# A hybrid state-space and attention layer on one core: the second block's row work moved ahead, its accumulators paired in two banks

## The chip, the cores and the metric

The kernel runs on one core of one Trainium2 chip. The time is device microseconds of one execution. Before the change three runs gave 1505.21, 1506.19 and 1507.15 us, median 1506.19. One execution was also taken by the hardware profiler; the numbers of the trace come from that one.

## The reference

One layer over 2048 rows of width 1024. The part that the change touches is the first: the rows are normalised and multiplied by the input weights, and the first 512 output columns (u) feed a state-space branch.

```python
hn = rmsnorm(h, mix_norm_g[i])
proj = hn @ w_in[i]
u, g_ssm, q, k, v, g_attn = jnp.split(proj, SPLITS, axis=-1)
y_ssm = s5_branch(u, ...)                     # diagonal complex scan, GELU, GLU
y_ssm = y_ssm * jax.nn.silu(g_ssm)
y_att = stick_breaking_branch(q, k, v, q_norm_g[i], k_norm_g[i]) * jax.nn.silu(g_attn)
h = h + jnp.concatenate([y_ssm, y_att], axis=-1) @ w_out[i]
ple_gate = jax.nn.sigmoid(rmsnorm(h, ple_norm_g[i]) @ w_ple_gate[i])
h = h + ple_gate * (p[i] @ w_ple_proj[i])
```

`rmsnorm` divides each row by the root of its mean square. All matrix products of the first phase are done in float32 split into a high and a low part: high by high, high by low, low by high, three matmuls for one product.

## The kernel before

**Stages.** `phase_u` computes u for all rows. A middle stage follows, in which the state-space batches (`ssm_pack`, `ssm_batch`), the gates (`gate_unit`) and the first attention projections are interleaved. Then come attention over four pairs of heads, the gated linear unit, and the two output products.

**phase_u.** The 2048 rows are taken in eight blocks T of 256 rows, each in two halves (hf) of 128. For each block the rows are needed transposed and split (tile `xt`), four accumulators `ps[ct]` take 24 matmuls each (8 column chunks by three parts, L541 to L543), and each is copied into `uq`.

- Block 0 comes from an input that already lies transposed (`load_plain`). It is not normalised before the product. Instead `norms(i)`, once for each half, squares the rows (L575), adds them up on POOL (L577) and with a matmul by ones (L579), raises the mean to -1/2 on POOL (L581), and spreads the factor along a row with a diagonal matrix `dg` and a second matmul (L585), which is copied to `row` (L586). Block 0's accumulators are multiplied by `row` on DVE when they are copied out.
- Blocks 1 to 7 are read as rows by `load_x(T)`: DMA into a tile `x` (L593), squares with a sum on ACT into `jk` (L596), the power on POOL (L507), scaling by it on ACT (L598), 16 transposes of 64 rows on PE (L526) into the two banks `z0` and `z1` (`ps_x`), and the split on ACT (L513, high) and DVE (L65, low). Their accumulators are copied out by ACT alone (L635).
- Four `x` tiles exist (`XB` is 4). The plain tiles of block 0 take two of them, block 1 the other two. Block 2 gets block 0's two, once the L579 matmuls have read them.

**Banks.** The accumulators of T=0 and of all later blocks lie in the banks `w0`, `w1`, `o` and `acc`, one each, 256 of 512 columns used. The row-factor matmuls use `tr` and `ssm`.

**What sets the order.** The code is only recorded. `arrange` then runs a list scheduler (`plan`, `list_schedule`, `best_order`) with its own durations, several turns, and fixes the order of the rows on each engine. `e.first()` pulls the rows recorded in it to the front of the ranking; `e.later(k)` makes the DMAs in it wait in the ranking for the place `e.mark(k)`. At equal rank, the program's order counts. The DMAs stand in the queue of SP. DVE also carries a long chain of small preparation operations for the state-space tables (`cm`, `tabs`, `pr_...`), which the scheduler threads between the splits.

## Time and profile before

| | |
|---|---|
| median of three runs | 1506.19 us (1505.21 to 1507.15) |
| the profiled execution's own time | 1509.53 us |
| its span, first to last instruction | 1507.8 us |
| granted TensorE clock, mean | 0.991 |
| ACT busy in 40 to 50 us | 7.48 of 10 us |
| DMA share in 30 to 40 us | 0.92 (338 GB/s) |

A timeline row reads: start, duration, engine, line, operation, tile written <- tiles read, shape, count, and in brackets the idle time of that engine just before, with what ended it. Rows with a count are merged. Start times of neighbouring matmuls are closer than their durations, since matmuls overlap; the step from one start to the next is what one costs in a stream.

### The profile page before, as it was taken

What the parts mean: (1) busy time and instruction counts of PE and PEld (TensorE: products, weight loads), DVE (VectorE), ACT (ScalarE), POOL (GpSimd) and SP (SyncE); (2) the same over time, 40 slices, a digit from 0 to 9 for tenths busy, and PEclk for the clock granted to TensorE, in tenths of its full rate; (3) what the DMA queues carried; (4) which work ended last, traced back from release to release, by engine and by line L of the source; (5) the groups of instructions that cost most, each with busy time, mean ns of one, the idle gap of its engine ahead of it and who ended that gap; (6) DMA issues with size and microseconds to landing.
All of it is one profiled execution on the core that took longest, in us unless ns stands there. A gap on an engine that the chain in (4) does not pass through costs nothing.

```text
span 1507.8 us, 33560 instructions
## 1 busy us (share of the span) xinstructions
PE 1455.0 (96%) x13068; PEld 1219.8 (81%) x13068; DVE 1012.1 (67%) x1802; ACT 810.9 (54%) x1764; POOL 483.4 (32%) x524
## 2 busy tenths in 40 slices
PE   5999999999999999999999989999998999999998
PEld 5999989988888888887888777787776888777776
DVE  8944878967667876676767775546687557744544
ACT  5654545566556765565655555646554435533332
POOL 3121354422212112211111343531245554433433
PEclk9999999999999999999999999999999999999999
DMA  8876736645333433334333577743376546423221
GB/s 290 285 270 231 228 131 199 192 156 190 118 113 129 149 111 109 126 119 128 107 116 123 163 231 205 222 147 93 105 243 216 177 162 203 154 65 112 76 68 58
DMA packets 178909, 238.21 MB, mean 158 GB/s; under 512 B 65744, under 2 KB 121024, under 8 KB 167616
## 3 DMA queue, kind: packets, MB, share of 16 engines
q1 hardware_dynamic: 176368, 227.49, 46.9%
q0 software_dynamic: 2384, 8.59, 2.0%
q8 instruction: 103, 1.69, 0.4%
q14 instruction: 54, 0.44, 0.1%
HBM read 166.94 MB, written 64.90 MB: 154 GB/s over the span
## 4 chain that ended last, share of the span: by engine, by line
PE 75%; DVE 11%; issue 5%; DMA 4%; ACT 3%; POOL 1%; SPq 0%; POOLq 0%; DVEq 0%; ACTq 0%
PE ps_q L745 20%; PE ps_o L843 7%; PE ps_z L812 6%; PE ps_wt L526 4%; PE ps_g L707 3%; PE ps_g L709 3%; PE ps_g L708 3%; PE ps_h L709 3%; PE ps_h L707 3%; PE ps_h L708 3%; DMA wst<-in_ssm_w_glu_dram 2%; PE ps_u L541 1%; PE ps_u L543 1%; PE ps_u L542 1%; PE ps_sg L541 1%
## 5 line engine op out<-in xcount | busy, mean ns | idle before, releaser
L821 DVE TENSOR_TENSOR_SCAN px<-px,ps_z 128x512 f32<-128x512 f32 (+3 forms) x320 | 338.9, 1085 | 112.0 <-ACT px L816 59.4
L745 PE MATMUL ps_q<-w_w,xt 64*128 64x512 f32 x2784 | 378.3, 401 | 0.0
L745 PEld LDWEIGHTS ps_q<-w_w,xt 64*128 64x128 f32 x2784 | 265.6, 186 | 44.8 <-DVE qn L65 0.9
L835 ACT ACTIVATE ws<-ps_wt 128x512 f32<-128x512 f32 (+3 forms) x320 | 160.3, 538 | 81.2 <-PE ps_wt L526 80.8
L816 ACT ACTIVATE px<-ps_z 128x512 f32<-128x512 f32 (+3 forms) x320 | 159.8, 535 | 68.3 <-PE ps_z L812 66.7
L812 PE MATMUL ps_z<-k,q 64*128 64x512 f32 (+3 forms) x960 | 140.7, 382 | 6.1 <-DVE px L821 5.9
L843 PE MATMUL ps_o<-ws,v 128*64 128x128 f32 x2176 | 137.1, 278 | 0.7 <-ACT ws L835 0.7
L507 POOL TENSOR_TENSOR rs_qk<-rs_qk,mhalf 128x4 f32<-128x4 f32 x64 | 67.6, 1057 | 208.7 <-DVE rs_qk L72 192.9
L843 PEld LDWEIGHTS ps_o<-ws,v 128*64 128x64 f32 x2176 | 118.8, 138 | 19.1 <-issue 13.9
L526 PEld LDWEIGHTS ps_wt<-ident,px 64*128 64x128 f32 x2176 | 96.7, 139 | 30.4 <-ACT ws L835 8.3
L526 PE MATMUL ps_wt<-ident,px 64*128 64x64 f32 x2176 | 103.1, 225 | 6.3 <-ACT ws L835 4.3
L812 PEld LDWEIGHTS ps_z<-k,q 64*128 64x128 f32 x960 | 87.4, 187 | 25.0 <-DVE px L821 8.0
L819 POOL TENSOR_SCALAR_AFFINE_SELECT px<-px 128x128 f32<-128x128 f32 x128 | 38.7, 312 | 169.0 <-ACT px L816 145.6
L541 PE MATMUL ps_u<-xt,w_w 128*128 128x256 f32 x256 | 75.0, 295 | 8.4 <-ACT w_w L491 7.0
L1015 POOL TENSOR_TENSOR sg<-sg,h 128x512 f32<-128x512 f32 x32 | 44.9, 1413 | 114.7 <-DVE sg L65 114.7
L756 POOL TENSOR_TENSOR v<-qn,v 128x128 f32<-128x128 f32 x64 | 30.3, 473 | 154.1 <-DMA v<-qn 133.2
L543 PE MATMUL ps_u<-xt,w_w 128*128 128x256 f32 x256 | 73.8, 294 | 2.6 <-DVE w_w L76 2.6
L65 DVE TENSOR_TENSOR yr<-sx,yr 128x512 fp32r<-128x512 f32 x64 | 52.9, 847 | 34.3 <-ACT yr L513 33.5
L542 PE MATMUL ps_u<-xt,w_w 128*128 128x256 f32 x256 | 74.3, 291 | 0.5 <-DVE xt L65 0.5
L65 DVE TENSOR_TENSOR qn<-ps_q,part 128x512 f32<-128x512 f32 x54 | 36.9, 683 | 45.4 <-ACT part L751 41.4
L513 ACT ACTIVATE yr<-sx 128x512 fp32r<-128x512 f32 x64 | 39.2, 628 | 52.1 <-POOL sx L901 20.7
L541 PEld LDWEIGHTS ps_u<-xt,w_w 128*128 128x128 f32 x256 | 50.9, 199 | 9.5 <-ACT w_w L491 7.6
(418 smaller groups left out, 3470.2 us busy)
## 6 DMA issues: line engine op xcount, KB each, us to landing
xt<-hn SPq DMA_DIRECT2D x58, 1024.0 KB
hn<-xt SPq DMA_DIRECT2D x16, 1024.0 KB
h<-h SPq DMA_DIRECT2D x64, 256.0 KB
wst<-in_w_in_dram SPq DMA_DIRECT2D x48, 256.0 KB
xg<-hn SPq DMA_DIRECT2D x12, 1024.0 KB
out_dram<-sg SPq DMA_DIRECT2D x32, 256.0 KB
x<-in_x_dram SPq DMA_DIRECT2D x14, 512.0 KB
h<-in_x_dram SPq DMA_DIRECT2D x28, 256.0 KB
```

The lines of the kernel that those rows point to most:

```text
L65: nc.vector.tensor_tensor(out, a, b, op=op)
L526: e.nc.tensor.transpose(ps[h][:, 64 * k:64 * k + 64], v[r], e.ident[r, r])
L541: mm(out, wh, xh, start=first, stop=False)
L707: mm(out, xh, wh, start=first, stop=False, skip_group_check=more)
L708: mm(out, xh, wl, start=False, stop=False, skip_group_check=more)
L709: mm(out, xl, wh, start=False, stop=last, skip_group_check=more)
L745: nc.tensor.matmul(o, xt[r, a, c], A.w[c][r, b], start=c + s == 0, stop=c == NC8 - 1 and s == 2)
L812: nc.tensor.matmul(z[:, :n], q[half[h], a], A.k[ch][half[h], b, :n], start=s == 0, stop=s == 2)
L816: nc.scalar.activation(px[:, :n], z[:, :n], AF.Sigmoid, scale=-(HD ** -0.5))
L821: nc.vector.tensor_tensor_scan(rv, rv, z[:, :n][:, ::-1], initial=1.0 if carry[h] is None else carry[h], op0=ALU.mult, op1=ALU.bypass)
L835: nc.scalar.activation(dst, ps, AF.Copy, bias=1.0, scale=-1.0)
L843: nc.tensor.matmul(po[half[h], :P], A.v[sb][:, h], w[:, h, b], start=sb == i, stop=sb == 0)
```

## The change

`load_x(1)` is called ahead of `norms(0)` and `norms(1)`. The row-factor matmuls go to the banks `z0` and `z1`, which the transposes use too. Block 1's four accumulators lie two to a bank, columns 0 to 255 and 256 to 511, in `tr` and `ssm`; the other blocks keep their four banks. No operation is added or taken away.

```diff
-        ps = e.bank("ps_row", "tr", "ssm")
+        ps = e.bank("ps_row", "z0", "z1")
         nc.tensor.matmul(ps[:, :1], x[:, 0], ones[:, :1], start=True, stop=True)
...
-        ps = e.bank("ps_row", "tr", "ssm")
+        ps = e.bank("ps_row", "z0", "z1")
         nc.tensor.matmul(ps[:, :P], ones, d, start=True, stop=True)
...
         xts[0], w = load_plain(0)
+        with e.later(0):
+            xts[1] = load_x(1)
         norms(0)
         norms(1)
-        with e.later(0):
-            xts[1] = load_x(1)
...
-        ps = [e.bank("ps_u", "w0", "w1", "o", "acc", *(("z0", "z1") if T < 1 else ()))[:, :256] for _ in range(4)]
+        if T == 1:
+            ps = [b[:, h:h + 256] for b in [e.bank("ps_u1", "tr", "ssm") for _ in range(2)] for h in (0, 256)]
+        else:
+            ps = [e.bank("ps_u", "w0", "w1", "o", "acc")[:, :256] for _ in range(4)]
```

The scheduler then sets another order. In these rows the number behind a tile's name tells its copies apart. Block 1's rows are `x_284` and `x_316` before and `x_258` and `x_290` after; block 2's are `x_886` and `x_918` in both; block 3's are `x_1055` and `x_1087` before, `x_1053` and `x_1085` after. Lines from L620 on have moved by 3 in the changed file, so the copy L635 is L638 there.

**PE at the opening of block 1.** Before, where the last products of block 0 give way to block 1 (the dots stand for more transposes of the same tiles):

```order
L543 MATMUL ps_u_784<-xt_188,w_w_250 128x256
L585 MATMUL ps_row_267<-dg_265,ones_186 128x128
L579 MATMUL ps_row_274<-ones_186,x_190 128x1
...
L585 MATMUL ps_row_280<-dg_278,ones_186 128x128
...
L541 MATMUL ps_u_950<-xt_283,w_w_197 128x256
L542 MATMUL ps_u_950<-xt_283,w_w_197 128x256
```

After the change:

```order
L526 MATMUL ps_x0_299<-ident_141,x_290 128x64
L526 MATMUL ps_x1_300<-ident_141,x_290 128x64
L579 MATMUL ps_row_326<-ones_186,x_189 128x1
L541 MATMUL ps_u1_950<-xt_257,w_w_197 128x256
L579 MATMUL ps_row_339<-ones_186,x_190 128x1
L542 MATMUL ps_u1_950<-xt_257,w_w_197 128x256
...
L585 MATMUL ps_row_332<-dg_330,ones_186 128x128
L541 MATMUL ps_u1_950<-xt_257,w_w_218 128x256
```

All four row-factor matmuls stood ahead of block 1's products, one of them (for `x_189`) inside block 0. Now they stand behind both groups of block 1's transposes, and the second L579 and both L585 inside block 1's first accumulator.

**ACT from block 1 to block 2.** Before:

```order
L596 ACTIVATE jk_920,ss_921<-x_918 128x1024
L598 ACTIVATE x_886<-x_886,rs_x_891 128x1024
L596 ACTIVATE jk_1057,ss_1058<-x_1055 128x1024
L635 ACTIVATE uq_777<-ps_u_950 128x16x16
L598 ACTIVATE x_918<-x_918,rs_x_923 128x1024
L513 ACTIVATE xt_885<-ps_x0_895 128x8x64
L513 ACTIVATE xt_885<-ps_x1_896 128x8x64
L635 ACTIVATE uq_778<-ps_u_951 128x16x16
```

After the change, with the semaphores that a row waits for:

```order
L638 ACTIVATE uq_777<-ps_u1_950 128x16x16 [waits PE_49]
L638 ACTIVATE uq_778<-ps_u1_950 128x16x16
L598 ACTIVATE x_886<-x_886,rs_x_891 128x1024 [waits Activation_49,Pool_49]
...
L638 ACTIVATE uq_779<-ps_u1_951 128x16x16 [waits PE_49]
L638 ACTIVATE uq_780<-ps_u1_951 128x16x16
L596 ACTIVATE jk_1055,ss_1056<-x_1053 128x1024 [waits DMAHW1_49,DVE_49,Activation_49]
L598 ACTIVATE x_918<-x_918,rs_x_923 128x1024 [waits Pool_49]
L596 ACTIVATE jk_1087,ss_1088<-x_1085 128x1024 [waits DMAHW2_49,DVE_49,Activation_49]
L513 ACTIVATE xt_885<-ps_x0_927 128x8x64 [waits PE_49]
L513 ACTIVATE xt_885<-ps_x1_928 128x8x64 [waits PE_49]
L598 ACTIVATE x_1053<-x_1053,rs_x_1058 128x1024 [waits Pool_49]
```

The scaling of block 2's first half stood ahead of block 1's copies and that of its second half behind the first copy. Now the first stands behind two copies and the second behind all four.

**PE between block 1 and block 2.** Before, the last product of block 1 and the first of block 2 were neighbours:

```order
L542 MATMUL ps_u_953<-xt_283,w_w_250 128x256
L543 MATMUL ps_u_953<-xt_283,w_w_250 128x256
L541 MATMUL ps_u_1119<-xt_885,w_w_197 128x256
L542 MATMUL ps_u_1119<-xt_885,w_w_197 128x256
L543 MATMUL ps_u_1119<-xt_885,w_w_197 128x256
```

After the change (each group of transposes has 16 rows, of which the first is shown):

```order
L542 MATMUL ps_u1_951<-xt_257,w_w_250 128x256
L543 MATMUL ps_u1_951<-xt_257,w_w_250 128x256
L526 MATMUL ps_x0_927<-ident_141,x_918 128x64
...
L526 MATMUL ps_x0_1062<-ident_141,x_1053 128x64
...
L541 MATMUL ps_u_1117<-xt_885,w_w_197 128x256
L542 MATMUL ps_u_1117<-xt_885,w_w_197 128x256
```

The transposes of block 2's second half, and those of block 3's first half, now stand between the two. From the first product of block 3 the count of PE's rows is the same in both programs.

On SP the loads of block 2's rows stood right behind the two writes of block 0's rows (`hn0`, `hn1`); now each stands behind a write of block 1's rows (`hn2`, `hn3`). On POOL the power for block 1's first half stood third behind the long additions and now stands first, ahead of the rest of `norms(1)`. On DVE the second split of block 2 now stands behind the preparation row `pr_t22i`; before, it stood 33 rows ahead of that row.

## The prediction

> **What bounds the kernel now.** I read the page first, for the engine that carries the run.
>
> ```profile
> span 1507.8 us, 33560 instructions
> PE 1455.0 (96%) x13068; PEld 1219.8 (81%) x13068; DVE 1012.1 (67%) x1802; ACT 810.9 (54%) x1764; POOL 483.4 (32%) x524
> ```
>
> TensorE is busy 1455.0 of 1507.8 us, so only 52.8 us of idle time can be won at all, and whatever makes it wait is paid in full. The change touches the first 100 us, so next I asked for the busy time by stretches. A row gives the stretch and its length, then the busy us of PE, PE's weight loads, DVE, ACT and POOL with their instruction counts, then the granted clock and the DMA share.
>
> ```profile
> 26.00:34.00 8.00, 3.53 (x41) 2.60 (x39) 8.00 (x37) 4.94 (x9) 2.73 (x5) 0.79 0.75 262
> 34.00:41.00 7.00, 6.48 (x30) 6.19 (x31) 6.98 (x43) 4.91 (x9) 1.91 (x2) 0.51 0.78 295
> 41.00:51.00 10.00, 10.00 (x104) 9.60 (x104) 8.83 (x49) 6.86 (x12) 1.23 (x2) 1.00 0.70 257
> 140.00:310.00 170.00, 166.96 (x1336) 157.02 (x1334) 143.07 (x248) 95.29 (x219) 73.09 (x42) 1.00 0.59 182
> ```
>
> Between the first and the second 256-row block (26 to 34 us) PE is idle for 4.5 of 8 us. Then it works at a granted clock of 0.51 for 7 us, and from 41 on it is never idle. DVE has no free time from 26 to 41 (8.00 of 8.00, 6.98 of 7.00). The timeline of PE gives the edges.
>
> ```profile
> 6.31 0.58 PE L541 MATMUL ps_u<-xt,w_w 128*128 128x256 f32 x1 [6.31 <-ACT w_w L491]
> 10.06 0.31 PE L542 MATMUL ps_u<-xt,w_w 128*128 128x256 f32 x1
> ...
> 28.42 0.71 PE L526 MATMUL ps_x<-ident,x 64*128 64x64 f32 x16 [0.38 <-ACT x L598]
> 31.51 1.12 PE L526 MATMUL ps_x<-ident,x 64*128 64x64 f32 x16 [1.67 <-ACT x L598]
> 33.80 0.58 PE L541 MATMUL ps_u<-xt,w_w 128*128 128x256 f32 x1 [1.18 <-ACT xt L513]
> 34.90 0.58 PE L542 MATMUL ps_u<-xt,w_w 128*128 128x256 f32 x1 [0.52 <-DVE xt L65]
> ...
> 41.54 0.28 PE L542 MATMUL ps_u<-xt,w_w 128*128 128x256 f32 x1
> 42.39 0.38 PE L543 MATMUL ps_u<-xt,w_w 128*128 128x256 f32 x1
> ...
> 50.51 0.28 PE L543 MATMUL ps_u<-xt,w_w 128*128 128x256 f32 x1
> ```
>
> The second block (T=1) opens at 33.80 and waits for its transposed, split rows (xt), from ACT and then from DVE, not for the row factors of T=0. The chain of waits, whose pieces do not overlap, gives the time of one product in this stretch:
>
> ```profile
> 40.60 0.21 PE ps_u L543
> 40.81 0.18 PE ps_u L541
> 40.99 0.12 PE ps_u L542
> ```
>
> Products step by 0.213 us until about 40.8 and by 0.12 after that. A group of 16 transposes between products makes a step of 0.85 (41.54 to 42.39) instead of 0.12, so it costs 0.73. By the order, 8 products of one accumulator and 24 of the last follow the second group of transposes, which puts the last product of T=1 at 50.51. T=2 follows at 50.63 without a gap, because its rows were loaded, squared, scaled and transposed inside T=1.
>
> **The change, part by part.** *Part 1, T=1 opens earlier.* These are the POOL, ACT, SP and DVE rows of the stretch.
>
> ```profile
> 25.39 0.58 POOL L581 TENSOR_TENSOR rs<-rs,mhalf 128x1 f32<-128x1 f32 x1
> 25.95 0.71 POOL L577 TENSOR_TENSOR x<-x 128x256 f32<-128x256 f32 x1
> 26.63 0.56 POOL L507 TENSOR_TENSOR rs_x<-rs_x,mhalf 128x1 f32<-128x1 f32 x1
> ...
> 27.22 1.15 ACT L598 ACTIVATE x<-x,rs_x 128x1024 f32<-128x1024 f32 x1 [2.16 <-POOL rs_x L507]
> 29.17 1.09 ACT L513 ACTIVATE xt<-ps_x 128x512 fp32r<-128x512 f32 x2 [0.64 <-PE ps_x L526]
> 30.29 1.16 ACT L598 ACTIVATE x<-x,rs_x 128x1024 f32<-128x1024 f32 x1
> 32.66 1.09 ACT L513 ACTIVATE xt<-ps_x 128x512 fp32r<-128x512 f32 x2 [1.21 <-PE ps_x L526]
> 33.63 1.06 ACT L596 ACTIVATE jk<-x 128x1024 bf16<-128x1024 f32 x1
> 34.81 1.06 ACT L596 ACTIVATE jk<-x 128x1024 bf16<-128x1024 f32 x1
> ...
> 40.21 0.39 ACT L635 ACTIVATE uq<-ps_u 128x256 f32<-128x256 f32 x1 [0.30 <-PE ps_u L543]
> 40.49 1.14 ACT L598 ACTIVATE x<-x,rs_x 128x1024 f32<-128x1024 f32 x1
> ...
> 24.70 4.86 SPq L593 DMA_DIRECT2D x<-in_x_dram  x3
> ...
> 31.11 0.57 DVE L65 TENSOR_TENSOR uq<-ps_u,row 128x256 f32<-128x256 f32 x1
> 33.57 1.27 DVE L65 TENSOR_TENSOR xt<-ps_x,xt 128x512 fp32r<-128x512 f32 x2
> 47.81 1.28 DVE L65 TENSOR_TENSOR xt<-ps_x,xt 128x512 fp32r<-128x512 f32 x2
> 55.28 1.28 DVE L65 TENSOR_TENSOR xt<-ps_x,xt 128x512 fp32r<-128x512 f32 x2
> 56.73 0.20 DVE L65 TENSOR_TENSOR pr_t22i<-cm,cm 128x32 f32<-128x32 f32 x1
> ```
>
> In POOL's new order the power of T=1's first half stands right behind the long additions, in the place at 25.39 instead of the one at 26.63, so the scaling L598 moves from 27.22 to 25.98. The transposes and splits follow at the same distances. The second scaling no longer stands behind a copy of the row factors and goes from 30.29 to about 28.9. DVE's split of the second half no longer stands behind the four T=0 products (31.11 to 33.57) and moves from 33.57 to about 31.9. L542 then comes at 33.5 rather than 34.90. I take a gain of 1.3 us, with bounds 1.0 and 1.6.
>
> The row factors' four matmuls leave the hole, where they cost nothing, and three of them now stand inside T=1's stream:
>
> ```profile
> L579 PE MATMUL ps_row<-ones,x x4: 250/260/272, 24.2 to 27.8; 128*128 128x1 f32 x4
> L585 PE MATMUL ps_row<-dg,ones x4: 275/311/377, 26.9 to 29.6; 128*128 128x128 f32 x4
> ```
>
> Each is two rows here, which overlap, so one L579 and two L585 cost between 0.26 + 2 x 0.31 = 0.9 and twice that, 1.8 us; they follow each other closely, and I take 1.1. The slow stretch at the opening lasted 3.75 us the first time (6.31 to 10.06) and 7.0 the second (33.80 to 40.8). If it is now between these, T=1 gains 0 to 1.4, because a slow us does only 0.12/0.213 = 56% of the work; I take 0.7. T=1 also holds one group of transposes instead of two, which is -0.73. T=1 therefore ends at 50.63 - 1.3 + 1.1 - 0.7 - 0.73 = 49.0.
>
> *Part 2, T=2 is no longer ready when T=1 ends.* Two things set it back. First, the x buffers of T=0 now come free late. They are read by the matmuls L579, which stood at 24 to 28 us and now stand behind T=1's transposes. So the loads of T=2's rows, which went out from 24.70 on, wait until about 33. Second, T=1's accumulators lie two to a bank, and in ACT's new order each pair is copied behind one wait; the second copy has none of its own. The copy of accumulators 0 and 1 thus waits for 48 products instead of 24, and ahead of the scaling of T=2's second half stand the copies of accumulators 2 and 3, which wait for the last product of T=1. ACT takes its rows in order, so from the end of T=1 this chain runs with PE waiting for it: 0.1 to reach ACT, two copies at 0.28 (40.21 to 40.49), one square at 1.18 (33.63 to 34.81), the scaling at 1.15, the next square at about 1.1 (it covers the transposes, 0.71), the two splits at 0.97 (32.66 to 33.63), and the scaling of T=3's first half at 1.15. In PE's order that half's transposes (0.85) stand ahead of T=2's first product. The sum is 0.1 + 0.56 + 1.18 + 1.15 + 1.1 + 0.97 + 1.15 + 0.85 = 7.1, which puts T=2 at 56.1.
>
> [...] If a copy could be given at its own half's end, one copy (0.28) would leave the chain and T=2 would start at 55.8.
>
> DVE may be later than ACT. Its new order puts the second split of T=2 behind the preparation row pr_t22i, which ended at 56.9. By then DVE had made two split pairs that the new order has not (47.81 and 55.28, 1.28 each), and it had idled about 1.2 us in 41 to 51 (8.83 busy of 10). If it never waits it is there at 56.9 - 2.6 - 1.2 = 53.1. With the waits that it gains for the row factors (they go DVE, POOL, DVE, PE, ACT while it stands, some 1 to 2.4 us) it is there at 54 to 55.5. Adding split and transposes (1.28 + 0.85), T=2 starts between 56.1 (ACT) and 57.6. I take 56.7, which is 6.1 later than 50.63. One more group of transposes has been done by then than before, which gives 0.73 back: 5.4 net.
>
> *Part 3, the clock.* Before T=1 PE had 7.8 us without products (26 to 33.8), with two groups of transposes in it, and came back at half speed. The new hole lasts from 49.0 to 56.7, 7.7 us, with two groups of transposes in it. So I let it come back slow again, for 3.75 to 7.0 us, of which 44% is lost: 1.65 to 3.1, and I take 2.3. If the clock holds, it is 0.
>
> [...]
>
> *Part 4, later.* In this place PE waited for DVE's splits before:
>
> ```profile
> 70.86 0.27 PE L526 MATMUL ps_x<-ident,x 64*128 64x64 f32 x1 [0.45 <-DVE xt L65]
> 71.46 0.71 PE L526 MATMUL ps_x<-ident,x 64*128 64x64 f32 x15 [0.33 <-DVE xt L65]
> ```
>
> A PE that comes 7 us later finds them done: -0.8. From T=3 on the order is nearly the old one up to the state-space stage. Between 140 and 310 gates, projections and state-space pieces are interleaved anew, with the same work. PE idles 3.0 of 170 us there, so a better order can win at most 3.0, and I allow as much for a worse one; I take 0. Behind it the orders agree apart from a few rows. The state-space work needs the last block's u, so it moves back with PE.
>
> Sum: +5.4 + 2.3 - 0.8 = +6.9 us. Against the profiled execution (1509.53, of which the span is 1507.8) that is 1516.4; its time is 3.3 above the median of the runs, 1506.19, which gives **1513.1**. The likeliest case's own range takes 2 us either way for the state-space stage: from 5.5 - 0.7 + 1.6 - 0.8 - 2 = +3.6 to 7.0 - 0.7 + 3.0 + 2 = +11.3, so 1509.8 to 1517.5.
>
> **The rivals.** *The hole closes (faster).* T=1's earlier opening is kept and T=2 follows at 49.0. It decides at one point: T=2's second scaling must be done when T=1's last product starts. Then 50.63 - 49.0 + 0.73 = 2.4 are won: 1503.8. With 0.6 of the 3.0 us in the state-space stage it is over 0.2%. For it: PE's 26 to 34 hole is real. Against it: ACT's order has two copies ahead of that scaling which wait for T=1's last product. Chance 0.05.
>
> *The delay is swallowed later (no change).* The state-space stage would have to be bound by DVE (143.07 of 170 us) rather than PE, so that 4 us or more are made up there: 1507 to 1509. Against it: PE idles only 3.0 us there. Chance 0.06.
>
> *The change does not do what it says (no change).* A planner sets the order by its own costs, so standing first in the program might move nothing: 1506. Against it: the new orders do differ, POOL's and PE's rows as said. Chance 0.04.
>
> *DVE sets a second hole.* DVE was without slack, and each wait that it now makes for the row factors also comes out in T=3's splits; a further hole like the first, with another slow stretch, adds 5 or more: 1518 to 1522. Against it: T=3's first half is transposed before T=2 begins. Chance 0.13.
>
> **How the numbers follow.** The likeliest case has 0.72. The range 1507.5 to 1518.5 holds it and part of the swallowed and the second-hole cases. About 0.2% (3 us) is what this measurement can tell from no change. Faster by more: 0.05. Within: 0.10. Slower by more: 0.72 + 0.13 = 0.85.
>
> **What would show it.** In the changed profile T=1's L542 should stand near 33.5, the loads of x behind 32, and T=1's last product near 49. PE should then be without products until 56.1 to 57.6, waiting for ACT's L598 and then DVE's xt, with ACT's two copies right behind T=1's end, and products at 0.213 once more behind it. If PE goes on into T=2 without a wait, Part 2 is wrong. If the steps behind the hole are 0.12, Part 3 is wrong. If the delay at T=3 is there and the end does not show it, the later stage is what I misjudged.

## The result, and the profile after

The changed kernel is slower: 1523.46 us, median of four runs (1519.95 to 1524.35), against 1505.70 of the kernel before on the same chip (1505.05 to 1507.15); ratio 1.0105, 95% interval 1.0089 to 1.0122. The forecast was 1513.1 with a range to 1518.5: the sign was right, the size was not. The profiled execution took 1523.60 us, 14.07 more than the profiled one before.

The first lines of the changed kernel's page:

```profile
span 1521.8 us, 33553 instructions
PE 1460.4 (96%) x13068; PEld 1225.1 (81%) x13068; DVE 1020.2 (67%) x1802; ACT 812.0 (53%) x1764; POOL 482.1 (32%) x524
```

PE has the same 13068 matmuls and is busy 5.4 us longer (at half speed a product steps by 0.21 us instead of 0.12); the rest of the 14 us is waiting. By stretches, with the columns as in the prediction (stretch, length, busy us of PE, weight loads, DVE, ACT, POOL, granted clock, DMA share, GB/s), after the change:

```profile
26.00:34.00 8.00, 3.07 (x37) 2.59 (x37) 6.32 (x34) 4.35 (x6) 2.11 (x4) 0.75 0.42 136
34.00:41.00 7.00, 7.00 (x49) 7.00 (x49) 5.68 (x23) 1.59 (x4) 0.69 (x2) 0.80 1.00 392
41.00:51.00 10.00, 7.31 (x70) 6.83 (x68) 10.00 (x68) 5.91 (x12) 1.32 (x2) 0.97 0.36 123
51.00:64.00 13.00, 9.02 (x84) 8.36 (x85) 12.64 (x57) 9.27 (x14) 1.93 (x3) 0.63 0.80 281
310.00:330.00 20.00, 16.32 (x127) 15.41 (x128) 14.80 (x32) 10.76 (x22) 2.76 (x4) 0.92 0.42 132
```

The first hole (26 to 34) is still there, a second one stands between 48 and 57.5, with the clock at 0.63 in 51 to 64, and there is a third place, 310 to 330, where PE works 16.32 of 20 us. The same stretch of time before (its rows are not the same ones; after the change they come 8 to 11 us later):

```profile
310.00:330.00 20.00, 18.43 (x188) 17.70 (x188) 11.38 (x21) 10.38 (x26) 2.99 (x8) 1.00 0.66 217
```

The timeline of PE between block 1 (T=1) and block 2 (T=2) after the change, with the ACT, DVE and SP rows that it waits for:

```profile
48.04 0.28 PE L543 MATMUL ps_u<-xt,w_w 128*128 128x256 f32 x1
51.91 1.12 PE L526 MATMUL ps_x<-ident,x 64*128 64x64 f32 x16 [3.60 <-ACT x L598]
55.93 0.34 PE L526 MATMUL ps_x<-ident,x 64*128 64x64 f32 x1 [2.89 <-DVE xt L65]
...
57.48 0.58 PE L541 MATMUL ps_u<-xt,w_w 128*128 128x256 f32 x1
57.85 0.41 PE L542 MATMUL ps_u<-xt,w_w 128*128 128x256 f32 x1
58.07 0.41 PE L543 MATMUL ps_u<-xt,w_w 128*128 128x256 f32 x1
...
48.35 0.66 ACT L638 ACTIVATE uq<-ps_u 128x256 f32<-128x256 f32 x2 [0.23 <-PE ps_u L543]
50.71 1.15 ACT L598 ACTIVATE x<-x,rs_x 128x1024 f32<-128x1024 f32 x1 [0.67 <-POOL rs_x L507]
...
54.99 0.19 DVE L65 TENSOR_TENSOR pr_t22i<-cm,cm 128x32 f32<-128x32 f32 x1
55.10 1.28 DVE L65 TENSOR_TENSOR xt<-ps_x,xt 128x512 fp32r<-128x512 f32 x2
...
33.66 12.74 SPq L593 DMA_DIRECT2D x<-in_x_dram  x4
...
46.98 1.06 ACT L596 ACTIVATE jk<-x 128x1024 bf16<-128x1024 f32 x1
49.61 0.19 DVE L72 TENSOR_SCALAR rs_x<-ss 128x1 f32<-128x1 f32 x1
49.90 0.78 POOL L507 TENSOR_TENSOR rs_x<-rs_x,mhalf 128x1 f32<-128x1 f32 x1 [5.89 <-DVE rs_x L72]
```

T=1's last product starts at 48.04, ACT's two copies right behind it, then the scaling (3.60 us of waiting for it on PE), then DVE's split, which stands behind pr_t22i as the order said (2.89 more). T=2 opens at 57.48, and its products step by about 0.21 (57.85 to 58.07): the clock is at half speed again (0.50 granted from 50.4 to 60.6 us).

The last three rows show what the scaling at 50.71 itself waited for last: POOL's power (0.67 us of ACT's idle time), behind a row of DVE, behind the square L596 of the same half at 46.98. That square waits for the load that went out at 33.66. By its semaphore that load had landed at 40.0, 7 us before the square began. So the square was late by its place in ACT's order, not because its data were missing. The load of the first half went out at 30.43, ahead of all L579 matmuls (the first starts at 32.77).

To follow the delay, the same PE instruction is looked up in both traces and its start before is subtracted from its start after. T=3's first product is 7.5 us late, a gate product that started at 138.5 is 6.2 late, a projection product that started at 380.2 is 12.2 late, and the end is 14.1 late. So the first phase costs 6.2 us, the middle stage 6.0, the rest 1.9. These are single executions: in the nine kernels of this study that have the changed order up to there, the delay at 138.5 is 6.2 to 7.6 us.

### The profile page after: what moved, and what is told of

It reads as the page before. It is cut to its first block, busy times and chain, and to the rows that moved or that the text cites. A ratio compares the mean times of both kernels' runs of the same rounds, so it can differ in the third digit from the quotient of the medians.

```text
span 1521.8 us, 33553 instructions
## 1 busy us (share of the span) xinstructions
PE 1460.4 (96%) x13068; PEld 1225.1 (81%) x13068; DVE 1020.2 (67%) x1802; ACT 812.0 (53%) x1764; POOL 482.1 (32%) x524
## 4 chain that ended last, share of the span: by engine, by line
PE 74%; DVE 9%; issue 4%; DMA 4%; ACT 4%; POOL 2%; SPq 1%; POOLq 0%; DVEq 0%; ACTq 0%
PE ps_q L748 20%; PE ps_o L846 7%; PE ps_z L815 6%; PE ps_wt L526 4%; PE ps_g L710 3%; PE ps_g L712 3%; PE ps_g L711 3%; PE ps_h L710 3%; PE ps_h L712 3%; PE ps_h L711 3%; PE ps_u L541 2%; PE ps_u L543 2%; PE ps_u L542 2%; DMA wst<-in_ssm_w_glu_dram 1%; PE ps_sg L543 1%
## 5 line engine op out<-in xcount | busy, mean ns | idle before, releaser
L748 PE MATMUL ps_q<-w_w,xt 64*128 64x512 f32 x2784 | 378.6, 402 | 1.5 <-DVE glus L76 1.4
L748 PEld LDWEIGHTS ps_q<-w_w,xt 64*128 64x128 f32 x2784 | 265.9, 186 | 47.0 <-DVE glus L76 1.8
L542 PE MATMUL ps_u<-xt,w_w 128*128 128x256 f32 x256 | 74.6, 293 | 0.0
```

The lines of the kernel that those rows point to most:

```text
L542: mm(out, wh, xl, start=False, stop=False)
L748: nc.tensor.matmul(o, xt[r, a, c], A.w[c][r, b], start=c + s == 0, stop=c == NC8 - 1 and s == 2)
```

## The experiments

**How an order was fixed.** Any edit makes the scheduler set a new order everywhere. To change one part alone, a kernel plans a second program with another set of the three edits, and takes from it the order of all rows that its own plan starts behind a seam:

```diff
-    _, order, _ = best_order(ops, pre, *rest, rows)
+    _, order, start = best_order(ops, pre, *rest, rows)
+    if tail is not None:
...
+        for q, line in order.items():
+            head = [k for k in line if start[k] < start[at]]
+            rest = [k for k in line if start[k] >= start[at]]
+            order[q] = head + sorted(rest, key=lambda k: tail[k])
...
+BEFORE = dict(first=False, row=("tr", "ssm"), pair=False)
+AFTER = dict(first=True, row=("z0", "z1"), pair=True)
```

`first` is the load order, `row` the banks of the row factors, `pair` the accumulators in pairs. `HEAD` is the kernel's own set of edits, `TAIL` the set of the second plan, and `tail` holds that plan's start times. The seam is block 3's first product unless another is named. "Price" below is the delay at the 380-us product less the delay at the 139-us product, "waits" the sum of PE's idle gaps over 0.15 us between the two, "half" the us at half-speed clock there. All three from the profiled execution, against the kernel before. The seams at 232 and 243 us were timed twice only.

| run | median us | ratio to before (95%) | delay at 139 | price | waits | half |
|---|---|---|---|---|---|---|
| before | 1505.7 | | 0 | 0 | 4.58 | 0 |
| the change | 1523.46 | 1.0105 (1.0089 to 1.0122) | 6.2 | 6.0 | 7.78 | 3.4 |
| new to block 3, old behind | 1514.45 | 1.0051 (1.0032 to 1.0070) | 7.7 | 0.4 | 4.94 | 0 |
| old to block 3, new behind | 1520.65 | 1.0093 (1.0078 to 1.0108) | 5.7 | 5.6 | 7.58 | 3.4 |
| load first, old behind | 1508.34 | 1.0014 (1.0001 to 1.0026) | 2.1 | 0.1 | 4.65 | 0 |
| banks alone, old behind | 1513.25 | 1.0043 (1.0028 to 1.0058) | 4.7 | 0.0 | 4.58 | 0 |
| without pairs, old behind | 1514.47 | 1.0053 (1.0034 to 1.0071) | 5.7 | 0.1 | 4.59 | 0 |
| load first, own order | 1513.42 | 1.0045 (1.0029 to 1.0062) | 5.6 | 0.7 | 5.74 | 0 |
| new to 195, old behind | 1514.03 | 1.0052 (1.0033 to 1.0071) | 6.9 | -1.3 | 3.50 | 0 |
| new to 232, old behind | 1521.90 | 1.0116 (1.0087 to 1.0146) | 7.0 | 6.9 | 9.18 | 6.8 |
| new to 243, old behind | 1522.90 | 1.0123 (1.0094 to 1.0152) | 7.6 | 7.7 | 8.99 | 6.8 |
| new to 250, old behind | 1522.29 | 1.0110 (1.0081 to 1.0139) | 6.2 | 6.7 | 10.25 | 6.8 |
| new to 303, old behind | 1522.81 | 1.0115 (1.0090 to 1.0141) | 7.0 | 5.0 | 8.85 | 0 |
| old to 195, new behind | 1522.26 | 1.0100 (1.0080 to 1.0120) | -0.1 | 14.9 | 11.98 | 13.7 |
| the change, small POOL rows | 1517.85 | 1.0088 (1.0057 to 1.0118) | 7.0 | 2.6 | 6.84 | 0 |
| before, small POOL rows | 1508.68 | 1.0006 (0.9989 to 1.0024) | 1.4 | 3.3 | 7.34 | 0 |
| the change, 33 gates later | 1520.96 | 1.0095 (1.0066 to 1.0124) | 6.4 | 6.0 | 8.35 | 3.4 |
| the change, 43 gates behind the batch | 1519.53 | 1.0098 (1.0077 to 1.0119) | 6.9 | 8.9 | 9.45 | 6.8 |

The kernel before, timed beside them, had medians from 1504.9 to 1507.6. In the rows of these kernels the lines behind about L600 carry numbers that are 8 to 13 higher than in the changed kernel (L748 is L756 or L761 there).

### First the two stages apart

**New order to block 3, old behind it.**

```diff
+HEAD, TAIL = AFTER, BEFORE
```

> The changed order on every engine up to the first product of block 3, the order of before from there on. It separates the two stages in which time was lost: about 6 us between T=1 and T=2, about 6 more between 140 and 330 us. Theory A (the new interleaving of the middle stage costs by its own): the delay stays near +6 from block 3 on and the middle stage adds -1 to +2; time 1505.7 + 6 + 0 to 4 = 1512 to 1516. Rival B (the delay of 6 us grows in the middle stage, whatever its order, because work that does not come from PE stays where it was): the delay is +10 to +13 at 340 us with the old order too, 1519 to 1524. If the delay at 340 us is below +4, the middle stage swallows part of it and the new order costs more than 6.

1514.45 us. The delay at T=3 is 8.8, at 139 us 7.7, at 380 us 8.1: with the old order the middle stage neither adds to an inherited delay nor swallows it. Theory A, and rival B is out.

**Old order to block 3, new behind it.** The same two sets, exchanged.

> The reverse: the order of before up to the first product of block 3, the changed order from there on. Theory A: no delay up to 140 us (within 1), +5 to +7 at 340 us, 1511 to 1515. Rival B: no delay at 140 us and none at 340 (within 2), 1504 to 1508. If both this kernel and the other half stay below +4 in the middle stage, it is the two together (the delay meets the new order) that costs the 6.

Price 5.6 without anything late in front of block 3, 1520.65 us. So the new order of the middle stage costs its 6 us by itself. Not as expected: the delay at 139 us is 5.7, not 0, and the time lies above the 1511 to 1515 of the theory. It arises at block 4, where PE waits 4.60 us for DVE's split at 74.4 and the clock falls for 6.8 us (0.80 granted in 64 to 80 us). The order has more preparation rows ahead of that split (28 DVE rows between it and the split before it, 23 in the kernel before); in the changed kernel, where block 2 is late, PE does not wait there. So the two parts do not add up: alone they cost 8.1 and 14.3 us, together 17.8.

### Which part of the change makes the first phase late

**Load first alone.**

```diff
+HEAD, TAIL = dict(first=True, row=("tr", "ssm"), pair=False), BEFORE
```

> Only the load, squares and scaling of block 1 stand first; row-factor matmuls in their old banks, block 1's accumulators in four banks; from block 3's first product on the order of before. Theory (the wait before T=2 comes from copies that wait for a pair's last product): here the scaling of block 2's second half stands behind the copy of the first accumulator alone, so T=2 opens within 1 us of T=1's last product, the clock comes back once only, and the delay at 100 us is -2 to +1; time 1503 to 1507. Rival (the late loads of block 2's rows alone hold T=2): 3 us or more without products between T=1 and T=2, delay +3 to +6, 1508.5 to 1513.

**Banks alone.**

```diff
+HEAD, TAIL = dict(first=False, row=("z0", "z1"), pair=True), BEFORE
```

> Only the banks: row-factor matmuls in z0 and z1, block 1's accumulators in pairs; load_x(1) in its old place; from block 3's first product on the order of before. The loads of block 2's rows go out early, and both scalings of block 2 stand ahead of all copies, but its second split stands behind the copies that wait for T=1's last product. Theory (pairs hold T=2 by the copies): from T=1's end 0.1 + two copies 0.56 + split 0.97 on ACT beside transposes 0.71 and the DVE split 1.28, then 0.85 for block 3's transposes: 2.0 to 3.5 us without products, too short for the clock to fall; T=1 opens at 33.8 as before or later by up to 1.3 (transposes behind the row factors' banks); delay at 100 us +2 to +4.5, time 1507.5 to 1511. Rival (pairs cost nothing by themselves while the loads are early): delay below +1, 1505 to 1507.

**Without the pairs.**

```diff
+HEAD, TAIL = dict(first=True, row=("z0", "z1"), pair=False), BEFORE
```

> The change without the pairs: load first, row factors in z0 and z1, block 1's accumulators in four banks; from block 3's first product on the order of before. The loads of block 2 are as late as in the change, and the scaling of its second half stands behind the copy of the third accumulator instead of the fourth's. Theory (the copies of a pair hold T=2): that copy is 24 products (2.9 us) earlier, so the wait for the scaling L598 shrinks from 3.6 us to under 1, T=2 opens 1.5 to 3 us after T=1's last product, the clock does not fall a second time, delay at 100 us +0.5 to +3, time 1506.5 to 1510. Rival (late loads and DVE's split hold T=2 whatever the copies): T=2 opens at 56 to 57.5 as in the change, delay +5 to +8, 1511.5 to 1515.

The timelines of PE at the end of T=1, first with the load first alone:

```profile
49.04 0.28 PE L543 MATMUL ps_u<-xt,w_w 128*128 128x256 f32 x1
49.16 0.28 PE L541 MATMUL ps_u<-xt,w_w 128*128 128x256 f32 x1
```

with the banks alone:

```profile
51.14 0.28 PE L543 MATMUL ps_u<-xt,w_w 128*128 128x256 f32 x1
...
54.51 0.27 PE L526 MATMUL ps_x<-ident,x 64*128 64x64 f32 x1 [1.93 <-DVE xt L65]
55.10 1.11 PE L526 MATMUL ps_x<-ident,x 64*128 64x64 f32 x15 [0.33 <-DVE xt L65]
56.14 0.58 PE L541 MATMUL ps_u<-xt,w_w 128*128 128x256 f32 x1
```

and without the pairs:

```profile
51.95 0.28 PE L543 MATMUL ps_u<-xt,w_w 128*128 128x256 f32 x1
...
54.04 0.38 PE L541 MATMUL ps_u<-xt,w_w 128*128 128x256 f32 x1 [1.17 <-ACT xt L513]
56.23 0.58 PE L542 MATMUL ps_u<-xt,w_w 128*128 128x256 f32 x1 [1.81 <-DVE xt L65]
```

With the load first alone T=2 follows without a gap, as expected. T=3 opens 0.5 us earlier than before, but at block 4 PE now waits 1.53 us for DVE's split at 71.43, and a half-speed stretch of 3.4 us follows (products step by 0.21 until 76.5), so the delay at 139 us is +2.1 and the time 1508.34, a little above the 1503 to 1507 expected. The earlier PE was worth nothing here, because DVE's split did not come earlier with it.

The banks alone leave 5.0 us without products (51.14 to 56.14), more than the 2.0 to 3.5 expected, with the clock falling once (products step by 0.21 until 58.2), and the time is above the 1507.5 to 1511 expected too. That 2.0 to 3.5 us would be too short for the clock to fall was the author's estimate; as a rule it is not shown: it fell behind waits of 1.53 and 0.33 us with the load first alone, and did not behind one of 2.81 us with the seam at 303 (1.00 in 310 to 330 us). T=1 also opens 2.4 us later (36.22): its transposes, which share z0 and z1 with the row factors, stand behind the last L585 (29.36), and from the second on (30.82) they waited 0.80 us for ACT's copy of a row factor.

Without the pairs the loads of block 2 go out as late as in the change (one DMA group of 13.57 us from 33.38 on). But here too the second half had landed (at 39.7) well before ACT squared it (at 47.52, by its order). The gap at T=2's second product is 4.3 us, half of the change's 9.4, and no scaling is waited for any more, only ACT's split (1.17) and DVE's (1.81). But T=1 opens 4 us late (37.73), because all four row-factor matmuls now stand ahead of it, and the delay is the rival's +5.7.

So the pairs are not needed for a gap, and neither is the early `load_x(1)`: each of the two kernels without one of them has a gap (4.3 and 5.0 us), the change has 9.4, and the load order alone has none. Both kernels with a gap have the row factors in z0 and z1, and no run has the pairs without that. In all three the last wait of the gap is for DVE's split. That the late loads hold T=2 is not shown; the two landing times speak against it (the planner may have set ACT's order as it did because it reckoned with them).

### The middle stage

**Load first, with the scheduler's own order behind.**

```diff
+HEAD, TAIL = dict(first=True, row=("tr", "ssm"), pair=False), None
```

> Only the load first, as in the run with the old order behind block 3, but with whatever order the scheduler itself sets from there on. The first phase is the same, so the delay at 60 us is -1 to +1. Theory (the middle stage's order is drawn anew by every change ahead of it, and its price has nothing to do with the delay): between 140 and 370 us the delay changes by some us although there is no delay to inherit, either sign, 1 us or more; where PE waits in the middle stage it is at the end of the state-space batches, for DVE's gsq, rot or sg. Rival (the new order costs because block 2 came late): the middle stage costs less than 1 us here. Time 1504 to 1516 by theory, 1504 to 1509 by the rival.

Price 0.7: the rival's side of the line, though a third order shows yet other waits (1.25 and 1.28 for rot). It loses 3.5 us elsewhere, between 80 and 100 us, where the same start with the old order behind it loses nothing. So this order went wrong in another stage.

**Seams inside the middle stage.** The changed order up to a place, the old one behind it, the seam moved to products that start at about 195, 232, 243, 250 and 303 us in the changed kernel, and once the reverse at 195. For 195 us (`CUT` counts the plan's matmuls):

```diff
+        pe = sorted((start[k], k) for k, op in enumerate(ops) if type(op).__name__ == "InstMatmult")
+        cut = start[at] if CUT is None else pe[CUT][0]
...
+HEAD, TAIL = AFTER, BEFORE
+CUT = 1420
```

> The changed order up to about 195 us (inside the second group of q and k products), the order of before from there on. Where does the middle stage lose its 6 us? Theory (by the order of the last batches: their DVE work comes late and too few gate products are left to cover it): with the old order from here on the middle stage adds 0 to 2 us, time 1513 to 1517. Rival (it is settled early, by how many gate products are done before the first batches end): 4 to 7 us, 1518 to 1523.

> The same with the seam at about 250 us. By the theory of the last batches the middle stage adds 0 to 3 us, 1513 to 1518; if it is settled between 195 and 250 us (DVE idles longer there in the changed kernel: busy 18.96 of 30 us in 200 to 230 against 22.48), 4 to 7 us, 1518 to 1523, with the loss in waits for DVE after 285 us.

> The mirror of the run with the changed order up to about 195 us: here the order of before up to the second group of q and k products, the changed order behind it. Nothing is late when it begins. Theory (the changed order behind 195 us has the price, by itself): no delay up to 195 us (within 0.5), PE's waits between 140 and 380 us are 7 to 8.5 us instead of 4.58, and the delay at 380 us is +4 to +7; time 1510 to 1514. Rival (the price needs both parts of the changed order, or a late block 2): waits below 5.5 us, delay at 380 us below +2, 1505 to 1509.

> The changed order up to about 303 us, that is up to the products of the next to last state-space batch; the order of before for what is left. Five waits of the changed kernel lie behind this place (0.22, 0.54, 0.53, 0.93 and 1.68 us, together 3.9 of its 7.78). Theory (too few gate products are left to cover the last batches' DVE work, since they were spent earlier): the old order cannot mend it, these waits stay at 3 us or more, the delay at 380 us stays at +10.5 to +13, 1520 to 1525. Rival (the last 25 us are merely ordered badly): the waits fall to 1.9 us or less (0.29 and 1.57 before), no slow clock at 327, delay +8 to +10, 1515 to 1520.

> The changed order up to about 232 us (the end of the third group of q and k products), the order of before behind it. With the seam at 195 the middle stage's price was -1.3 us, with the seam at 250 and 303 it was 6.7 and 5.0. If the price is settled between 195 and 232 us (the fourth state-space batch's first scan on DVE, 8.5 us later than before at 230.8): price +4 to +7, with waits of PE behind 232 us of 6 us or more. If it is settled behind 232 us: price below +2.5, waits below 5.5 us in all.

> The same with the seam at about 243 us. If the price is settled before 232 us, +4 to +7 as with the seam there; if between 232 and 243 us, +4 to +7 here and below +2.5 with the earlier seam; if behind 243 us, below +2.5 in both.

PE's largest waits at the end of the stage, a row with its idle time before it in brackets, first in the kernel before:

```profile
300.04 0.49 PE L464 MATMUL ps_y<-rot,stC 128*128 128x127 f32 x2 [0.66 <-DVE rot L65]
306.06 0.46 PE L461 MATMUL ps_y<-us,tp 128*128 128x128 f32 x2 [0.29 <-DVE gsq L65]
316.62 0.97 PE L745 MATMUL ps_q<-w_w,xg 64*128 64x512 f32 x6 [1.57 <-DVE gsq L65]
```

in the changed kernel:

```profile
295.36 0.64 PE L347 MATMUL ps_pack<-bn,cts 128*32 128x256 f32 x8 [0.94 <-ACT stB L341]
311.13 0.49 PE L464 MATMUL ps_y<-rot,stC 128*128 128x127 f32 x2 [0.54 <-DVE rot L65]
317.39 0.49 PE L461 MATMUL ps_y<-us,tp 128*128 128x128 f32 x2 [0.53 <-ACT tp L455]
324.24 0.55 PE L815 MATMUL ps_z<-k,q 64*128 64x128 f32 x6 [0.93 <-DVE sg L65]
326.47 4.61 PE L748 MATMUL ps_q<-w_w,xg 64*128 64x512 f32 x24 [1.68 <-DVE gsq L65]
369.85 0.58 PE L526 MATMUL ps_wt<-ident,px 64*128 64x64 f32 x12 [0.85 <-ACT g L794]
```

with the old order behind 195 us:

```profile
305.38 0.49 PE L464 MATMUL ps_y<-rot,stC 128*128 128x127 f32 x2 [0.65 <-DVE rot L65]
321.96 0.97 PE L756 MATMUL ps_q<-w_w,xg 64*128 64x512 f32 x6 [1.57 <-DVE gsq L65]
```

and with the new order behind 195 us and the old one ahead of it:

```profile
312.68 0.49 PE L464 MATMUL ps_y<-rot,stC 128*128 128x127 f32 x2 [0.54 <-DVE rot L65]
318.94 0.49 PE L461 MATMUL ps_y<-us,tp 128*128 128x128 f32 x2 [0.53 <-ACT tp L455]
325.79 0.55 PE L823 MATMUL ps_z<-k,q 64*128 64x128 f32 x6 [0.93 <-DVE sg L65]
328.02 5.49 PE L756 MATMUL ps_q<-w_w,xg 64*128 64x512 f32 x24 [1.68 <-DVE gsq L65]
```

The kernel before has most of the waiting at 311 to 326 too: between 300 and 330 us its waits are 2.5 us together, the changed kernel's 3.9. Of the 3.2 us of waits that the change adds in the whole stage, 1.4 lie there, 0.94 are the wait at 295 and 0.85 the one at 370, both for ACT's rows.

Two readings hold. With the old order from 195 us on the price is gone (-1.3). With the new order from 195 us on the four waits at 311 to 326 are those of the changed kernel to the hundredth (those at 295 and 370 come back as 0.95 and 0.85), though no block was late. The seam itself makes a wait of 3.45 us at 198 with a half-speed stretch of 6.8, and the stretch at 327 lasts 6.8 instead of 3.4, so that kernel's price of 14.9 is not the order's. The changed order behind 195 us thus has the waits, whatever stands ahead of it. The seams at 232, 243, 250 and 303 all keep a price of 5.0 to 7.7. But each has a large wait of its own at or behind the seam (3.78 us for DVE's qn, 3.45 for rot, 6.41 for bn, 2.81 for rot) instead of the four waits at 311 to 326; the 1.57 of the kernel before is there again in all four. That fits an order that is already behind in DVE's work at 232, as expected of it, and it also fits two orders that do not match at a seam. These four runs do not tell the two apart.

**POOL's long rows cut.**

```diff
-    gp(cview, pw(R.pr, 1, False), st(R.cts), op=ALU.mult)
-    gp(tm2, pw(R.pi, 1, False), st(R.ct2), op=ALU.mult)
-    gp(cview, cview, tm2, op=ALU.subtract)
+    if e.v.get("small") and b >= 2:
+        nc.scalar.activation(cview, st(R.cts), AF.Copy)
+        gp(tm2[:, :1, :1], pw(R.pi, 1, False)[:, :1, :1], st(R.ct2)[:, :1, :1], op=ALU.mult)
+        gp(cview[:, :1, :1], cview[:, :1, :1], tm2[:, :1, :1], op=ALU.subtract)
...
+HEAD, TAIL = dict(AFTER, small=True), AFTER
```

All rows keep the order of the kernel without this cut; the kernel before takes `BEFORE` in both places.

> The changed kernel in its own order throughout, but in the six later state-space batches POOL's three long rows per batch (the products for stC, 2.1 to 2.9 us each) are cut: stC is filled by one copy on ACT instead, and POOL multiplies and subtracts 16 of 1024 columns. In the changed kernel DVE rows that usually take 0.2 to 1.2 us take up to 3.3 beside such POOL rows; above each row's median that is 33.6 us in 140 to 350 us, against 28.9 before. Theory (the new order's price is DVE time lost beside POOL, for which PE waits behind 285 us): the lost DVE time falls below 18 us here and in the kernel of before with the same cut, and the middle stage's price (this kernel's delay at 370 us less its delay at 140 us, against the kernel of before with the same cut) falls from 6 to 0 to 2.5 us. Rival (the price is the order of the batches' pieces itself, whatever POOL does): it stays at 4 to 7 us. Times 1516 to 1520 by the theory, 1520 to 1524 by the rival.

> The kernel of before in its own order with the same cut of POOL's rows; the base for the kernel beside it. Both theories: DVE's lost time falls below 18 us; PE waited 3.0 us in 140 to 310 us and 1.57 at 316, so 0 to 3 us can be won: 1503 to 1506.5. The difference between the two kernels, 17 us so far: 11 to 14 by the theory, 15 to 18 by the rival.

DVE's time above each row's median in 140 to 350 us falls from 35.9 to 10.9 us in the changed kernel and from 32.1 to 7.5 in the one before (medians over these four kernels, rows of one operation, tiles and shape together). The price between the two falls to -0.7, and their medians lie 9.2 us apart instead of 17.8; the theory had 0 to 2.5 and 11 to 14, the rival 4 to 7 and 15 to 18. That looks like the theory's success, but it is not clear that it is one. The edit moves work to ACT, and the kernel before became 3.3 us worse in this stage: its waits rose from 4.58 to 7.34, and of five new ones three, 1.8 us together, are for ACT's rows. And in the changed kernel the last waits stand as they were:

```profile
323.38 0.55 PE L828 MATMUL ps_z<-k,q 64*128 64x128 f32 x6 [0.93 <-DVE sg L65]
325.61 3.01 PE L761 MATMUL ps_q<-w_w,xg 64*128 64x512 f32 x24 [1.68 <-DVE gsq L65]
```

DVE's time lost beside POOL does not make these two waits. Of the 3.3 us that the changed kernel won, 0.9 are waits (above all the one for ACT's stB, 0.94 at 295, of which 0.20 for another row of ACT is left) and 1.5 the half-speed stretch at 327, which is missing here. Whether the rest of the price comes from DVE's lost time stays open.

**Gate products moved.** In every kernel with the changed order at 205 to 220 us DVE idles 5.46 us for q. Rows were moved on PE, with the ACT and DVE rows that read them, and nothing else:

```diff
+    held = [k for k in pe[i:j] if out(k).startswith("ps_sg")][30:]
+    for n, k in enumerate(held):
+        key[k] = start[pe[end]] + 1e-6 * (n + 1)
...
+    for line in order.values():
+        line.sort(key=lambda k: key[k])
```

The second run takes `pe[i:end]` instead, which is 10 gate products more.

> The changed kernel in its own order, with one thing moved. In every kernel that has the changed order at 205 to 220 us, DVE stands idle for 5.46 us at 209.8, waiting for q: PE has 63 gate products ahead of the transposes for it and of the state-space products on which DVE's following rows wait. Here the last 33 of these gate products (4.0 us at 0.12) stand behind those transposes and state-space products, with the one ACT row and the one DVE row that read them. Theory (this idle time of DVE puts its state-space work behind, and PE pays for it in the waits after 285 us): DVE's wait for q falls to 1.5 us or less, PE's waits between 139 and 380 us fall from 7.8 to 4.5 to 6 us, the middle stage's price from 6.0 to 1 to 3.5 us, time 1517 to 1521. Rival (the later pieces are ordered badly in themselves): DVE's wait falls as well, but PE's waits stay at 7 us or more and the price at 5 us or more, 1521.5 to 1525.

> The changed kernel in its own order, with the last 33 of the 63 gate products at 206 to 214 us and the 10 behind them moved further than in the run before: behind all products that feed the fourth state-space batch (its second pack and its products ps_b, which end at 222.6 us in the changed kernel and at 213.3 before); the rows of ACT and DVE that read these gates stand behind the batch's first scan on DVE. That scan starts at 230.8 us in the changed kernel, 8.5 later than before, though PE is only 6.2 behind. Theory (the lateness of this batch's input, behind 43 gate products, is the price): the scan starts at 225.5 to 228, PE's waits between 139 and 380 us fall from 7.8 to 4.5 to 6 us, the price from 6.0 to 1 to 3.5 us, time 1517 to 1521. Rival (the later batches are spaced badly by themselves: their first scans stand 23.8, 13.6, 28.7 and 10.6 us apart, before 21.2, 19.4, 20.3 and 16.6): the scan is early, the last scans are not, waits 7 us or more and price 5 us or more.

DVE's waits of over 2 us at this place, in the changed kernel:

```profile
215.22 0.29 DVE L65 TENSOR_TENSOR q<-ps_tq,q 128x128 fp32r<-128x128 f32 x1 [5.46 <-ACT q L513]
```

and with 33 gates later:

```profile
212.38 0.29 DVE L65 TENSOR_TENSOR q<-ps_tq,q 128x128 fp32r<-128x128 f32 x1 [2.45 <-ACT q L513]
...
219.76 0.42 DVE L65 TENSOR_TENSOR sg<-ps_sg,sg 128x256 f32<-128x256 f32 x1 [3.40 <-ACT sg L670]
```

The wait for q shrank, the moved gates made one of 3.40 us behind it, 5.85 together, and the price stayed at 6.0. So this move did not take DVE's idle time away, and tests the theory only in part. With 43 gates behind the whole input of the fourth batch, its first scan came at 229.2 instead of 230.8, not as early as the 225.5 to 228 that the theory asked for, while T=3 was 0.7 later than in the change. The later scans came 2.6 us later than in the change, and the price rose to 8.9, of which the doubled half-speed stretch at 328 is 1.5. That is the rival's outcome: an earlier fourth batch did not bring the later ones forward. Neither move lowered the price, and neither theory is supported.

## Why the prediction missed, step by step

**Part 1 was right in its steps, not in its gain.** The two scalings came at 26.03 and 28.95 (25.98 and 28.9 predicted) and DVE's split at 31.93 (31.9). But L542 came at 34.09 (33.5 predicted, 34.90 before), a gain of 0.8, below the lower bound of 1.0: one of the three row-factor matmuls that the sum priced apart stood ahead of it. T=1 nevertheless ended a microsecond earlier than forecast (last product at 48.04, 49.0 taken for the end). From L542 on it took 1.66 us less than before. The clock, at half speed until 36.8 instead of 40.8, gave 1.4 of this (0.7 taken), the missing group of transposes 0.73, and the row-factor matmuls cost about 0.5 (1.1 taken). The hole became 9.3 us instead of 7.7, since DVE and not T=1's end set where it closes.

**Part 2 was right about the place and the opening, and only in part about the causes.** T=2 opened at 57.48, at DVE's end of 56.1 to 57.6 (56.7 taken), and DVE's split came behind pr_t22i at 55.10, as said. ACT's two copies stood where the forecast had them. But the scaling behind them waited last for POOL's power, and the late loads are not shown to have held anything: the first went out at 30.43, ahead of the first L579, so it cannot have waited for the tiles of block 0 as the forecast had it, and the second half had landed 7 us before its square.

**Part 3 was right in kind.** The clock was at half speed from 50.4 to 60.6, so products lost 44% of 3.1 us, 1.4 (2.3 taken, 1.65 the lower bound): 7.1 of the 10.2 us at half speed fell into the hole. At T=3 the delay was 7.5, where Parts 1 to 3 had 7.7; that an opening 0.8 later and a half-speed loss 0.9 smaller cancelled is luck.

**Part 4 is where it failed.** Its first term, 0.8 us won back at 70 us, held in kind: those waits are gone, and the delay fell by 1.3, from 7.5 at T=3 to 6.2 at 139 us, against a forecast sum of 6.9. The step "Between 140 and 310 gates, projections and state-space pieces are interleaved anew, with the same work ... I take 0", with 2 to 3 us either way, is the mis-sized term: from 138.5 to 380 us it measured +6.0. The bound was drawn from PE's 3.0 us of idle time, as if a worse order could lose only what a better one could win; but idle time has no such upper bound. It also ended too early: at 310 us of the kernel before the two orders still differ, and agree only from about 328 us on, but for short stretches. By then 4.7 of the 6.0 are there, and the wait of 0.85 at 370 comes behind it.

Of the 6.0, 3.2 are waits (7.78 against 4.58), about 1.5 is a half-speed stretch of 3.4 us that follows two of them, and 1.2 is spread over steps too small to list. Shown is that the new order behind 195 us has these waits by itself. More than half of the added waiting (0.94 and 0.85 of 3.2 us) is for rows of ACT, and no run moved those alone. That the two largest waits come from DVE's time lost beside POOL is refuted; that moving the gates ahead of the fourth batch would mend the stage found no support. Which rows of that order are at fault stays open.

**Two terms were not in the sum.** Behind 380 us 1.9 us were lost although the order is the same but for a few rows: the traces show 20.8 us at half speed there instead of 16.3, and 44% of the difference is 2.0. The other 16 kernels have nearly the same order there too, and against the same trace they took between 4.7 us less and 0.3 more. So one execution differs from another by more than these 1.9 us, and that the change causes them is not shown. The mean clock moves from run to run as well (0.985 to 0.988 for the change, 0.987 to 0.996 for the kernel before). And the sum was shifted down by 3.3 us because the profiled execution of before lay that far above its median; the profiled execution of the change lies on its median (1523.60 and 1523.46), so nothing was there to shift, and the forecast came out lower by these 3.3 us.

Against the profiled execution: 6.9 - 0.7 (first phase) + 6.0 + 1.9 = 14.1. Against the medians 3.7 more, 17.8: before's profile lies 3.83 above its median, the change's 0.14. So 12.2 of the 17.8 us have a place in the order of the rows; the other 5.6 have none.

**The rivals.** The hole did not close, the delay was not swallowed (0.4 us of change with the old order, twice 0.1), and DVE set no second hole in T=3 of the changed kernel (it did at block 4 with the old order ahead of the new one). What came was a loss in the stage that no rival named. The sign that the prediction gave for this, a delay at T=3 that the end does not show, is what was seen, in the other direction.

## What to carry to other kernels

Where a planner sets the order, an edit in one stage redraws the order of the others, and the price of that is a term of its own: bound it on the losing side by more than the idle time that can be won, or fix the order behind the edit and measure the edit alone (here 8 of the 18 us). Here two accumulators in one bank were copied together at the second one's end (48.35), and the rows that the next block needed stood behind these copies in ACT's order; look for such rows before pairing. A transfer that goes out late is a cause only if its reader waits for it: compare the landing with the reader's start (here 40.0 and 46.98). Compare a sum made on one profiled execution with the spread of the runs before shifting it to their median.

## What the hardware did that was not expected

Apart from those that the end of a run cuts off, the half-speed stretches in the profiled executions of the two kernels (four before, seven after the change) last 3.41, 6.83 or 10.24 us, and within one execution all of them start on one grid of 3.413 us, to 2 ns. The column "half" of the table has nothing but 0, 3.4, 6.8 and 13.7 us. One of 3.4 us followed waits of 0.93 and 1.68 us that together are shorter than itself. The windows of the changed kernel at that place:

```profile
320.00:323.40 3.40, 3.31 (x30) 3.10 (x28) 2.09 (x4) 1.28 (x3) 0.00 (x0) 1.00 0.77 232
323.40:326.80 3.40, 0.88 (x9) 0.76 (x11) 2.95 (x5) 3.00 (x7) 0.35 (x1) 1.00 0.33 119
326.80:330.20 3.40, 3.40 (x20) 3.20 (x18) 0.93 (x3) 0.00 (x0) 0.60 (x2) 0.51 0.87 252
```

PE was busy 0.88 of 3.40 us, and the clock was 0.51 for the next 3.40. With POOL's rows cut the same two waits stood 0.9 us earlier, PE was busy 2.47, 1.72 and 3.40 us of the same three stretches (4.19 of the first two together, as in the changed kernel), and the clock was 1.00 in all of them. Counted on the grid of each of the two traces, from 60 to 1490 us: the two full-speed steps of the grid in which PE was busy for less than 0.46 of the step (0.45 from 1133.1 us before, 0.28 from 323.5 after the change) were followed by half speed, none of the 811 over 0.64 was, and in between both occurred (before, 0.59 from 873.7 was followed by it, 0.47 from 853.2 was not).

A DVE row took ten times as long beside a POOL row. The rows of POOL and DVE in the changed kernel:

```profile
283.96 2.70 POOL L334 TENSOR_TENSOR stC<-stC,tm 128x1024 f32<-128x1024 f32 x1
284.52 2.23 DVE L65 TENSOR_TENSOR dg<-ident,dsk 32x64 f32<-32x64 f32 x1
...
291.27 0.22 DVE L65 TENSOR_TENSOR dg<-ident,dsk 32x64 f32<-32x64 f32 x1
```

The same 64 columns take 0.22 us alone and 2.23 beside a POOL row, ending 0.09 us after it (286.75 and 286.66). That 25 us of DVE's time above the medians could be taken away in the kernel before (32.1 to 7.5 us) without a gain (ratio 1.0006, with the copy on ACT in its place) was the surprise.
